# Block attention of a decoder trunk: transposes of q, k and three groups' probabilities by VectorE blocks and on-chip transfers

## The chip, the cores and the metric

The kernel runs on one core of a Trainium2 chip. The core has a matrix engine (TensorE, PE; its weight loads are listed as PEld), VectorE (DVE), ScalarE (ACT), GpSimd (POOL) and SyncE (SP), which here only issues transfers. Each engine works through a fixed list of instructions in order; semaphores make one wait for another. Transfers are issued on queues of SP, ACT and POOL and carried out by 16 DMA engines. The on-chip memory (SBUF) has 128 partitions; PE writes to banks of a second memory, PSUM.

The metric is device time in microseconds (us), the median of the runs; the profile is of one execution.

## The reference

A trunk of two layers on one sequence of 256 positions, width 1024, all in float32. Each layer is half a SwiGLU FFN (width 2816), a token mixer, and another half FFN; each part has an RMS norm with a shift, a scale and a gate worked out from a vector c (here called modulations). The mixer of layer 0 is the block attention (16 heads of 64) that the change touches; that of layer 1 has its own low-rank attention and is left as it is.

```python
def moba_attention(h, w_qkv, q_g, k_g, w_o, rel_bias, positions):
    qkv = (h @ w_qkv).reshape(B, S, 3, H, Dh)
    q = rms_norm(qkv[:, :, 0], q_g).transpose(0, 2, 1, 3)
    k = rms_norm(qkv[:, :, 1], k_g)
    v = qkv[:, :, 2]
    ...
    s = jnp.einsum("bhqd,bhqnkd->bhqnk", qc, kg).astype(jnp.float32) * scale + bias.astype(jnp.float32)
    mask = (kidx <= qi[None, None, :, None, None]) & sv[None, None, :, :, None]
    s = jnp.where(mask, s, NEG)
    p = jax.nn.softmax(s.reshape(B, H, QC, nslot * L), axis=-1).reshape(s.shape).astype(vg.dtype)
    return jnp.einsum("bhqnk,bhqnkd->bhqd", p, vg)
    ...
    return o @ w_o
```

The block length is 256, the whole sequence, so what remains is causal attention over 256 keys with a bias by relative position.

## The kernel before

**Precision and weights.** Every large matrix product is made of three: each float32 operand is split in a high part (rounded to the faster float32r) and a low part (the rest), and high x high, high x low and low x high are summed in PSUM (`mm3`, lines 898 to 900). A weight tile (`wload`) comes from DRAM on SP's queue into `raw` (three buffers of 1 MB), ScalarE writes its high part `hi` (line 690), VectorE the low part `lo` (line 691), 1024 columns at a time, into eight buffers each. So all weights pass through ScalarE and VectorE too. The function `weight_tiles` fixes the order in which they come.

**Modulations.** VectorE also multiplies the modulation matrices with c, in units of one 512 KB tile `adaw` (lines 705 and 746; line 746 for the gates). They are spread over the stages by `ada_pace`, with a time to spread them over (`MOBA_PACE`, 98, in the block attention).

**The order of instructions.** The Python program emits the work in one order, helped by a clock of TensorE time: `pe(us)` moves the clock, `later(us, fn)` emits `fn` when the clock has moved so far, `until(cond)` emits what is pending until the condition holds. Then the class `Order` lays out every engine's list anew: it works out how long each instruction takes (`duration`), when it is needed (`needs`), and places all instructions one by one on five engines (`place`), with the buffers of each pool, a model of the DMA engines, and at most eight transfers of SP in flight. TensorE takes the earliest emitted instruction that is ready, the others the one needed first. `NUDGE` shifts four single instructions in this.

**Block attention (`moba`).** The heads go in four groups g of four (`GH`). `project` makes q and k of a group (512 columns) for a tile t of 128 positions (two tiles); `qk` normalises each head (squares on ScalarE, sum on VectorE at line 1309, the power -1/2 on GpSimd at line 1310, a multiply on VectorE at line 1458) into `qn`; `vals` makes v of two groups at once. The order is q/k of group 0 and v of groups 0 and 1, q/k of 1, v of 2 and 3, q/k of 2, q/k of 3. `to_T` transposes `qn` on TensorE (line 1478, eight 128x128 transposes per group) into PSUM, and ScalarE copies them out with the gains (line 1480) as `qT` and `kT`.

**One group (`attention`).** `scores` makes q times k into four PSUM banks (line 1206), VectorE adds the bias and finds the row's limit (line 1223), ScalarE takes exponentials with their sum (line 1230), VectorE multiplies by the reciprocals (line 1236). `transposes` turns the probabilities on TensorE (line 1245, twelve per group) and ScalarE copies them out as `pT` (line 1247). `av` multiplies with v (line 1271). For the first three groups `av` is kept (`glued`) and emitted at the head of the next group's `scores`. `load_bias` fetches the next group's bias on POOL's queue into its one buffer. At the end `out_proj` multiplies by the output weights in eight pieces of four k-slices; the first three pieces need groups 0 and 1 alone.

**Names of the instructions in the profile:** `tr` and `at` are PSUM tiles, `s` the probabilities, `bg` the bias, `h` and `oT` the split inputs of projections.

## Time and profile before

| | |
|---|---|
| median of 3 runs | 976.41 us (975.74 to 977.19) |
| the profiled execution, first to last instruction | 973.7 us |
| median less that span | 2.7 us |
| TensorE busy | 966.8 us, 99% |
| VectorE busy | 833.7 us, 86% |
| ScalarE busy | 597.9 us, 61% |
| GpSimd busy | 81.4 us, 8% |
| moved by DMA | 268.31 MB, mean 276 GB/s |

The page gives, for one execution, the busy time of each engine, 40 slices of the span, the DMA queues, the chain of work that ended last (followed back from the last instruction, at each step to what released it), the costliest groups of instructions by source line, and the DMA issues with their time to landing. The trace behind it is asked for windows of time, for the waits, the chain in order of time, and the timeline. A group's row reads: line, engine, operation, output<-input, shapes, count | busy us, mean ns of one | idle time of the engine before them and what ended it. TensorE's matmuls overlap, so the mean of one (about 390 ns) is longer than the distance from one to the next (about 228 ns).

The order of the stages: first FFN to about 207 us, block attention with its output projection to about 320 us, second FFN to about 507 us, the next layer's first FFN to about 700 us, then the second attention and, from about 790 us, the last FFN.

### The profile page before, as it was taken

Reading aid. Unit: us, or ns where it says so; the run is one execution under the profiler, and the core shown is the slowest. Engines: PE = TensorE matmul, PEld = TensorE weight load, DVE = VectorE, ACT = ScalarE, POOL = GpSimd, SP = SyncE. Lnnn points to the kernel's source line nnn. Section 1 sums busy time; section 2 is a strip of 40 time slices with the busy share of each in tenths; the row PEclk is TensorE's granted clock in tenths of the full one; section 3 lists DMA queues with packets and bytes.
Section 4 is the critical chain, followed back from the end, with each engine's and each line's share of the span. In section 5 each row is a group of like instructions: output and inputs, shape, how many; then the busy total and the mean of one; then the engine's idle time right before and its main releaser. Section 6 shows DMA issues by size and latency. Waiting matters only on the chain.

```text
span 973.7 us, 15174 instructions
## 1 busy us (share of the span) xinstructions
PE 966.8 (99%) x5562; PEld 829.1 (85%) x5566; DVE 833.7 (86%) x1397; ACT 597.9 (61%) x1082; POOL 81.4 (8%) x130
## 2 busy tenths in 40 slices
PE   8999999999999999999999999999999999999998
PEld 6998888888887888888888888888998888888887
DVE  7999999799999999999797699988998789666643
ACT  5689655377766955655367566543689696665521
POOL 2001100022230000000010000000142000000000
PEclk9999999999999999999999999999999999999999
DMA  9987989799887699999887598997634367545630
GB/s 355 408 339 262 335 314 384 281 359 360 303 302 246 226 351 348 331 327 346 318 306 269 191 345 330 362 373 241 202 120 165 131 259 276 200 173 195 237 131 22
DMA packets 56002, 268.31 MB, mean 276 GB/s; under 512 B 6638, under 2 KB 7864, under 8 KB 38008
## 3 DMA queue, kind: packets, MB, share of 16 engines
q1 hardware_dynamic: 53136, 259.23, 71.9%
q0 software_dynamic: 2352, 7.77, 2.5%
q8 instruction: 44, 0.72, 0.3%
q10 hardware_dynamic: 440, 0.34, 0.1%
q14 instruction: 30, 0.25, 0.1%
HBM read 263.09 MB, written 4.23 MB: 275 GB/s over the span
## 4 chain that ended last, share of the span: by engine, by line
PE 95%; DVE 2%; POOL 1%; DMA 1%; issue 1%; ACT 0%; SPq 0%; DVEq 0%; ACTq 0%
PE mm L1112 26%; PE mm L898 15%; PE mm L899 15%; PE mm L900 15%; PE mm L1120 14%; PE at L1198 1%; PE at L1245 1%; PE tr L1374 1%; POOL hr L1310 1%; PE at L1271 1%; PE mm L1847 1%; PE tr L948 1%; PE tr L1657 1%; PE mm L1848 1%; PE mm L1849 1%; PE tr L1847 1%
## 5 line engine op out<-in xcount | busy, mean ns | idle before, releaser
L691 DVE TENSOR_TENSOR lo<-raw,hi 128x1024 fp32r<-128x1024 f32 (+2 forms) x302 | 358.5, 1207 | 84.4 <-ACT hi L690 79.1
L690 ACT ACTIVATE hi<-raw 128x1024 fp32r<-128x1024 f32 (+2 forms) x302 | 305.9, 1044 | 137.1 <-PE mm L900 100.0
L1112 PE MATMUL mm<-h,hi 128*128 128x512 f32 x1104 | 266.7, 392 | 0.0
L1112 PEld LDWEIGHTS mm<-h,hi 128*128 128x128 f32 x1104 | 202.1, 188 | 39.1
L1120 PEld LDWEIGHTS mm<-h,lo 128*128 128x128 f32 x1104 | 142.5, 191 | 5.7
L1120 PE MATMUL mm<-h,lo 128*128 128x256 f32 x1104 | 145.5, 283 | 0.0
L705 DVE CUSTOM_DVE_ANT_0 adaw<-adaw,c_b,cols 128x1024 f32<-128x1024 f32 (+1 forms) x112 | 140.2, 1269 | 0.3 <-DMA adaw<-in_ada_dram 0.2
L898 PE MATMUL mm<-hi,gh 128*128 128x512 f32 (+1 forms) x356 | 138.2, 389 | 0.0
L899 PE MATMUL mm<-lo,gh 128*128 128x512 f32 (+1 forms) x356 | 137.9, 387 | 0.0
L900 PE MATMUL mm<-hi,gl 128*128 128x512 f32 (+1 forms) x356 | 137.6, 387 | 0.0
L1124 ACT ACTIVATE both<-mm 128x256 f32<-128x256 f32 x108 | 40.6, 380 | 99.3 <-PE mm L1120 99.1
L898 PE MATMUL mm<-hi,h 128*128 128x512 f32 (+2 forms) x256 | 98.2, 389 | 0.0
L899 PE MATMUL mm<-lo,h 128*128 128x512 f32 (+2 forms) x256 | 98.1, 385 | 0.0
L900 PE MATMUL mm<-hi,h 128*128 128x512 f32 (+2 forms) x256 | 97.6, 385 | 0.0
L900 PEld LDWEIGHTS mm<-hi,gl 128*128 128x128 f32 x356 | 66.9, 188 | 13.6
L899 PEld LDWEIGHTS mm<-lo,gh 128*128 128x128 f32 x356 | 66.9, 188 | 13.1
L898 PEld LDWEIGHTS mm<-hi,gh 128*128 128x128 f32 x356 | 66.8, 188 | 13.1
L746 DVE CUSTOM_DVE_ANT_0 adaw<-adaw,c_b,cols 128x1024 f32<-128x1024 f32 x48 | 60.5, 1278 | 0.0
L898 PEld LDWEIGHTS mm<-hi,h 128*128 128x128 f32 x256 | 48.0, 188 | 9.2 <-issue 1.2
L900 PEld LDWEIGHTS mm<-hi,h 128*128 128x128 f32 x256 | 48.0, 188 | 8.5 <-DVE h L914 0.2
L899 PEld LDWEIGHTS mm<-lo,h 128*128 128x128 f32 x256 | 48.1, 188 | 8.1
L1125 DVE TENSOR_TENSOR both<-both,mm 128x256 f32<-128x256 f32 x108 | 43.8, 417 | 9.5 <-ACT both L1124 9.3
(264 smaller groups left out, 1148.5 us busy)
## 6 DMA issues: line engine op xcount, KB each, us to landing
raw<-in_w_dram SPq DMA_DIRECT2D x140, 1024.0 KB, 5.6
adaw<-in_ada_dram SPq DMA_DIRECT2D x158, 512.0 KB, 5.7
raw<-in_w_dram SPq DMA_DIRECT2D x14, 512.0 KB, 4.3
raw<-in_first_dram SPq DMA_DIRECT2D x7, 512.0 KB, 9.6
raw<-in_first_dram SPq DMA_DIRECT2D x9, 384.0 KB, 9.6
bias_d<-bt SPq DMA_DIRECT2D x12, 256.0 KB, 6.2
gate<-gate_d POOLq DMA_DIRECT2D x6, 512.0 KB, 7.6
bg<-bias_d POOLq DMA_DIRECT2D x4, 768.0 KB, 7.1
```

The costliest lines, as they stand in the source:

```text
L690: nc.scalar.activation(hi, src, AF.Copy)
L691: nc.vector.tensor_tensor(lo, src, hi.bitcast(F32), op=ALU.subtract)
L705: nc.vector.tensor_tensor_reduce(wt[:, cs], wt[:, cs], c_b[:, cs], 1.0, at, op0=ALU.mult, op1=ALU.add, accum_out=m_cols[:, i, c:c + 1])
L746: nc.vector.tensor_tensor_reduce(wt, wt, c_b, 1.0, places["gates"][:, c:c + 1], op0=ALU.mult, op1=ALU.add, accum_out=g_cols[:, row, k:k + 1])
L898: nc.tensor.matmul(ps, lh, rh, start=start, stop=False)
L899: nc.tensor.matmul(ps, lh, rl, start=False, stop=False)
L900: nc.tensor.matmul(ps, ll, rh, start=False, stop=stop)
L1112: nc.tensor.matmul(ps, wh, hk_both(h, k).rearrange("p i t q -> p (i t q)"), start=k == 0, stop=False)
L1120: nc.tensor.matmul(ps[:, S:], wl, hk_both(h, k)[:, 0].rearrange("p t q -> p (t q)"), start=False, stop=k == KD - 1)
L1124: nc.scalar.activation(sums, ps[:, S:], AF.Copy)
L1125: nc.vector.tensor_tensor(sums, sums, ps[:, :S], op=ALU.add)
L1847: nc.tensor.matmul(ps, wh, hh, start=False, stop=False)
```

## The change

The q, k and the probabilities of groups 0 to 2 are no longer turned by TensorE. VectorE transposes all 32x32 blocks of a [128, 512] tile in one instruction (`turn_blocks`, reading every fourth element, so that the four rows of partitions that belong together end up side by side), and four transfers from SBUF to SBUF (`move_blocks`) carry the 32 partitions of each quarter to all 128. The q/k moves are issued on ScalarE's queue, the moves of probabilities on SP's. Group 3's probabilities are still turned by TensorE.

- The gains of q and k are multiplied into one vector and applied to q alone; ScalarE writes the scaled q into the buffer of the blocks, k is read where the transfer left it, in runs of 32 elements.
- In the turned groups the probabilities are scaled by ScalarE, one head at a time, instead of by VectorE.
- The probabilities, their blocks and the moved copy share one tag of two buffers of 128x1536 instead of five of 128x512; v has one buffer of two groups instead of two.
- The projections go q/k of 0, v of 0 and 1, q/k of 1, 2, 3, v of 2 and 3; the weights come in that order.
- `Order` follows access patterns over partitions, gives on-chip transfers a duration of their own, and counts only SP's transfers as in flight; the nudges are gone. The waits before `scores` (`SQ_WAIT`) and the pace of the modulations in this stage change.

```diff
+AVT_WAIT = 9.0
+SQ_WAIT = 12.0
+TURN_LAST = False
...
-MOBA_PACE = 98.0
+MOBA_PACE = 86.0
...
-                for g in (0, -1, 1, -2, 2, 3):
+                for g in (0, -1, 1, 2, 3, -2):
...
-NUDGE = ((6613, 30), (6710, 100), (6712, 10), (6762, -100))
+NUDGE = ()
...
+                if self.aps[k][0].tensor.space == self.aps[k][-1].tensor.space:
+                    dur = min(dur, 2200.0 + 2.0 * self.transfer(k) + (1500.0 if e == "Pool" else 0.0))
...
-                if e != "Pool":
+                if e == "SP":
                     flight.append(t + dur)
...
+    def turn_blocks(z, x):
+
+        nc.vector.transpose(z.rearrange("p j n b -> p n j b"), x.rearrange("p (n a j) -> p n j a", j=4, a=NB))
+
+    def move_blocks(queue, xT, z):
+
+        X = math.prod(z.shape[2:])
+        for i in range(4):
+            queue.dma_start(xT[:, i].rearrange("p n b -> p (n b)"), z[i * NB:(i + 1) * NB].rearrange("a j n b -> a (j n b)"))
...
+        turned = bias is not None and (g < NG - 1 or TURN_LAST)
...
+            if bias is not None:
+                whole_s.append(ap.tile([P, 4, 3 * GH, NB], F32, tag="w", name=nm("s"), bufs=2).rearrange("p i n b -> p (i n b)").rearrange("p (u c) -> p u c", c=512))
...
-                nc.vector.tensor_tensor(ss[u], ss[u], rs[:, :n, None].to_broadcast([P, n, P * (t + 1)]), op=ALU.mult)
+                if turned:
+                    for i in range(n):
+                        nc.scalar.activation(ss[u][:, i, :], ss[u][:, i, :], AF.Copy, scale=rs[:, i:i + 1])
+                else:
+                    nc.vector.tensor_tensor(ss[u], ss[u], rs[:, :n, None].to_broadcast([P, n, P * (t + 1)]), op=ALU.mult)
             state["s"] = g + 1
-            later(PT_WAIT, transposes)
+            if not turned:
+                later(PT_WAIT, transposes)
+                return
+            z, w = [ap.tile([P, 4, 3 * GH, NB], F32, tag="w", name=nm(n), bufs=2) for n in ("zP", "pT")]
+            for u in range(len(us)):
+                turn_blocks(z[:, :, u * GH:(u + 1) * GH, :], ss[u].rearrange("p e k -> p (e k)"))
+            move_blocks(nc.sync, w, z)
...
-        later(S_WAIT, scores)
+        later(S_WAIT if bias is None else SQ_WAIT, scores)
...
-                    v[g] = v[g + 1] = ap.tile([P, NT, 512], F32, tag="v", name=nm("v"), bufs=2)
+                    v[g] = v[g + 1] = ap.tile([P, NT, 512], F32, tag="v", name=nm("v"))
...
-                for i in range(2):
-                    pt = tr_tile()
-                    for t in range(NT):
-                        for j in range(GH // 2):
-                            nc.tensor.transpose(kslice(pt, 2 * j + t), kslice(qn[g, t], 2 * i + j), ident)
...
+                z = ap.tile([P, 4, 2 * GH, NB], F32, tag="zqk", name=nm("zqk"))
+                qkT = ap.tile([P, 4, 2 * GH, NB], F32, tag="qkT", name=nm("qkT"))
+                for t in range(NT):
+                    turn_blocks(z[:, :, t * GH:(t + 1) * GH, :], qn[g, t])
+                move_blocks(nc.scalar, qkT, z)
+                blocks = qkT.rearrange("p i (t n) b -> p t n i b", t=NT)
+                qT = z.rearrange("p j n b -> p (j n b)")[:, :GH // 2 * S].rearrange("p (t n q) -> p t n q", t=NT, q=P)
+                for t in range(NT):
+                    nc.scalar.activation(qT[:, t].rearrange("p n (i b) -> p n i b", b=NB), blocks[:, t, :GH // 2], AF.Copy, scale=gain)
...
-            for fn, g in ((qk, 1), (vals, 2), (qk, 2), (qk, 3)):
+            for fn, g in ((qk, 1), (qk, 2), (qk, 3), (vals, 2)):
```

More of the change, by code (lines that the diff above doesn't have):

```diff
@@ L350, in add @@
                     p0 = ap.offset // size
-                    p1 = p0 + ap.ap[0][1]
-                    key = ap.offset % size, tuple(tuple(d) for d in ap.ap[1:])
+                    p1 = p0 + 1 + sum(d // size * (c - 1) for d, c in ap.ap if d >= size)
+                    key = ap.offset % size, tuple(tuple(d) for d in ap.ap if d[0] < size)
                     if key not in masks:
@@ L1181, in attention @@
     def attention(ap, g, qTs, kTs, vs, bias, oT, state, after_s=None):
-        pT, ss, sms = {}, [], []
+        pT, ss, whole_s = {}, [], []
+        turned = bias is not None and (g < NG - 1 or TURN_LAST)
         us = UNITS if bias is None else SIDES
@@ L1212, in scores @@
             mxs = []
-            for (t, es), ps in zip(us, banks):
+            if bias is not None:
+                whole_s.append(ap.tile([P, 4, 3 * GH, NB], F32, tag="w", name=nm("s"), bufs=2).rearrange("p i n b -> p (i n b)").rearrange("p (u c) -> p u c", c=512))
+            for u, ((t, es), ps) in enumerate(zip(us, banks)):
                 nk = P * (t + 1)
-                s3 = ap.tile([P, 512], F32, tag="w", name=nm("s"), bufs=5).rearrange("p (e k) -> p e k", k=nk)
+                s3 = whole_s[0][:, u] if whole_s else ap.tile([P, 512], F32, tag="w", name=nm("s"), bufs=5)
+                s3 = s3.rearrange("p (e k) -> p e k", k=nk)
                 mx = small([P, 4], "mx")
@@ L1235, in scores @@
                 nc.vector.reciprocal(rs[:, :n], sm[:, :n])
-                nc.vector.tensor_tensor(ss[u], ss[u], rs[:, :n, None].to_broadcast([P, n, P * (t + 1)]), op=ALU.mult)
-            state["s"] = g + 1
-            later(PT_WAIT, transposes)
+                if turned:
[3 more added lines that the diff above has]
+                    nc.vector.tensor_tensor(ss[u], ss[u], rs[:, :n, None].to_broadcast([P, n, P * (t + 1)]), op=ALU.mult)
+            state["s"] = g + 1
+            if not turned:
[5 more added lines that the diff above has]
+            move_blocks(nc.sync, w, z)
+            for u, (t, es) in enumerate(us):
+                for i, e in enumerate(es):
+                    for kb in range(t + 1):
+                        pT[t, e, kb] = w[:, :, u * GH + i * (t + 1) + kb, :]
+            turned_in()
         def transposes():
+            if whole_s:
+                pw = ap.tile([P, 4, 3 * GH, NB], F32, tag="w", name=nm("pT"), bufs=2)
+                pw = pw.rearrange("p i n b -> p (i n b)").rearrange("p (u c) -> p u c", c=512)
             for u, (t, es) in enumerate(us):
@@ L1245, in transposes @@
                         nc.tensor.transpose(kslice(pt, i * (t + 1) + kb), ss[u][:, i, kb * P:(kb + 1) * P], ident)
-                w = ap.tile([P, 512], F32, tag="w", name=nm("pT"), bufs=5)
+                w = pw[:, u] if whole_s else ap.tile([P, 512], F32, tag="w", name=nm("pT"), bufs=5)
                 nc.scalar.activation(w, pt, AF.Copy)
@@ L1253, in transposes, with turned_in @@
             pe(1.4)
+            turned_in()
+        def turned_in():
             state["p"] = g + 1
@@ L1259, in transposes @@
             else:
-                later(AV_WAIT, lambda: av([1] if g == NG - 1 else [0, 1]))
+                later(AVT_WAIT if turned else AV_WAIT, lambda: av([0, 1] if turned or g < NG - 1 else [1]))
         def av(ts):
@@ L1427, in moba @@
             load_bias(0)
-            gains = {n: places[n] for n in ("moba_q", "moba_k")}
-            nc.vector.tensor_scalar(gains["moba_q"], gains["moba_q"], -DH ** -0.5, None, op0=ALU.mult)
-            qT = ap.tile([P, GH // 2, S], F32, name="qT")
+            gain = places["moba_q"]
+            nc.vector.scalar_tensor_tensor(gain, gain, -DH ** -0.5, places["moba_k"], op0=ALU.mult, op1=ALU.mult)
             oTp = ap.tile([P, KD, 2, NT, P], F32R, name="oT")
@@ L1472, in to_T @@
                 until(lambda: state.get("s", 0) >= g)
-                kT = ap.tile([P, GH // 2, S], F32, tag="kT", name=nm("kT"))
-                for i in range(2):
-                    pt = tr_tile()
-                    for t in range(NT):
-                        for j in range(GH // 2):
-                            nc.tensor.transpose(kslice(pt, 2 * j + t), kslice(qn[g, t], 2 * i + j), ident)
-                    pv = pt.rearrange("p (j q) -> p j q", j=GH // 2)
-                    nc.scalar.activation((qT, kT)[i], pv, AF.Copy, scale=gains[("moba_q", "moba_k")[i]])
-                pe(0.9)
-                def half(x, e, n0, n1):
-                    return x[e % 2 * DH:(e % 2 + 1) * DH, e // 2, n0:n1]
+                z = ap.tile([P, 4, 2 * GH, NB], F32, tag="zqk", name=nm("zqk"))
[7 more added lines that the diff above has]
+                    nc.scalar.activation(qT[:, t].rearrange("p n (i b) -> p n i b", b=NB), blocks[:, t, :GH // 2], AF.Copy, scale=gain)
+                rows = lambda x, e: x[e % 2 * DH:(e % 2 + 1) * DH]
                 attention(
                     ap, g,
-                    lambda e, t: half(qT, e, t * P, (t + 1) * P),
-                    lambda e, n: half(kT, e, 0, n),
+                    lambda e, t: rows(qT, e)[:, t, e // 2],
+                    lambda e, n: rows(blocks, e)[:, :n // P, GH // 2 + e // 2],
                     lambda e, kb: v[g][:, kb, (g % 2 * GH + e) * DH:(g % 2 * GH + e + 1) * DH],
```

## The prediction

> **What bounds the kernel now.** I read the page first: the engines' busy time and the chain that ended last.
>
> ```profile
> PE 966.8 (99%) x5562; PEld 829.1 (85%) x5566; DVE 833.7 (86%) x1397; ACT 597.9 (61%) x1082; POOL 81.4 (8%) x130
> ...
> PE 95%; DVE 2%; POOL 1%; DMA 1%; issue 1%; ACT 0%; SPq 0%; DVEq 0%; ACTq 0%
> ```
>
> TensorE (PE) is busy in 966.8 of 973.7 us and holds 95% of the chain. An average hides the stages, so next come windows: the block attention with its output projection (207 to 320), the start of the second FFN, the rest of that FFN's first part, and its down projection with the next FFN's first matmuls. Columns: stretch, length, then busy time of PE, PEld, VectorE (DVE), ScalarE (ACT) and POOL, granted clock, DMA share, GB/s.
>
> ```profile
> 207.00:320.00 113.00, 112.84 (x646) 91.65 (x645) 106.69 (x213) 81.92 (x172) 24.96 (x16) 1.00 0.83 302
> 320.00:344.00 24.00, 24.00 (x113) 19.67 (x113) 21.96 (x35) 21.93 (x42) 1.48 (x1) 1.00 0.73 275
> 344.00:445.00 101.00, 101.00 (x584) 89.15 (x583) 97.26 (x145) 59.01 (x92) 2.23 (x4) 1.00 0.91 338
> 445.00:529.00 84.00, 84.00 (x382) 69.36 (x381) 70.11 (x96) 47.31 (x73) 2.94 (x2) 1.00 0.82 302
> ```
>
> In the stage of the change PE idles 0.16 us in 113: time comes off only if PE work comes off. But VectorE idles just 6.3 us there and 3.7 us in the next 101, and the DMA engines are 83% and 91% busy. PE gets relief; the work goes to the two resources with the least room. Then the chain of waits, in order of time (start, length, what), inside the stage:
>
> ```profile
> 232.23 0.87 PE tr L1478 x8
> ...
> 235.85 1.51 PE at L1206 x16
> ...
> 237.79 0.23 PE mm L899
> ...
> 243.03 1.31 PE at L1245 x12
> ...
> 256.15 1.51 PE mm L1271 x24
> ...
> 300.37 1.51 PE at L1206 x16
> ...
> 310.93 1.08 PE at L1271 x16
> ```
>
> These are, for one group of four heads: q/k transposes, scores, one matmul of a projection, transposes of the probabilities, their product with v; then the last group's scores and final product.
>
> **The change part by part.** The groups of instructions of the stage (207 to 325), one row for each shape: busy us, mean ns | idle before.
>
> ```profile
> L746 DVE CUSTOM_DVE_ANT_0 adaw<-adaw,c_b,cols 128x1024 f32<-128x1024 f32 x8 | 10.0, 1278 | 0.0
> ...
> L1236 DVE TENSOR_TENSOR s<-s,rs 128x512 f32<-128x512 f32 x12 | 8.2, 691 | 0.3
> ...
> L1247 ACT ACTIVATE pT<-at 128x512 f32<-128x512 f32 x12 | 6.6, 597 | 2.8 <-PE at L1245 2.8
> ...
> L943 ACT ACTIVATE y<-x,rstd 128x256 f32<-128x256 f32 x8 | 3.6, 495 | 0.0
> ...
> L1480 ACT ACTIVATE qT<-tr,cols 128x512 f32<-128x512 f32 x4 | 2.8, 689 | 2.6 <-PE tr L1478 2.6
> L1480 ACT ACTIVATE kT<-tr,cols 128x512 f32<-128x512 f32 x4 | 2.7, 681 | 0.0
> ...
> L913 ACT ACTIVATE h<-y 128x128 fp32r<-128x128 f32 x5 | 1.5, 307 | 0.1
> ```
>
> *PE, removed.* The q/k transposes of all groups go, four blocks of 0.87 (x8), and those of three groups' probabilities, three blocks of 1.31 (x12). 3.48 + 3.93 = 7.4 us, all on the path: PE has no idle time to absorb them. *PE, changed.* Scores and products now read moving operands in runs of 32 elements. No row shows such a matmul. Bounds: nothing, or twice the blocks of 1.51 (four of scores, three of products: +10.6 us). I take nothing, since the element count is unchanged and every matmul row here goes by its count.
>
> *VectorE.* Removed: nine of the twelve multiplies L1236, 9 x 0.69 = 6.2. Added: 2 block transposes for each of four groups and 3 for each of three, 17 of 128x512. The trace has none. The nearest row of that size is L1236 itself, 0.69; I take it: 11.7, net +5.5. The reads step over four elements, so the ceiling comes from two reductions of the same 128 elements, strided (L1343) and contiguous (L1356):
>
> ```profile
> L1343 DVE TENSOR_REDUCE own<-ident 128x32 f32<-128x128 f32 x1 | 0.4, 374 | 0.0
> ...
> L1346 DVE CAST posq<-posi 128x256 f32<-128x256 int32 x1 | 0.3, 285 | 0.0
> L1356 DVE TENSOR_REDUCE blk<-ident 128x4 f32<-128x128 f32 x1 | 0.3, 272 | 0.0
> ```
>
> 102 ns more over 128 elements is 0.8 ns for each; over 512, +0.41: 1.10 apiece, 18.7 in all, net +12.5. The floor is twice the conversion of 256 elements (row L1346), 0.57: 9.7, net +3.5. At 0.69 the stage asks VectorE for 106.7 + 5.5 = 112.2 us where PE now asks for 105.4. The cover is the modulation work of L746, 10.0 us for a gate that is read only behind the next FFN's down projection; 445 to 529 has 13.9 us of VectorE idle to take it. If it isn't put off, 6.8 us land on the path.
>
> [...]
>
> *ScalarE.* Removed: 8 x 0.69 (L1480) + 9 x 0.60 (L1247) = 10.9. Added: 8 scaled q copies at L943's 0.495 = 4.0; 24 scalings of the probabilities, 12 x 0.307 and 12 x 0.495 = 9.6; the issue of 16 transfers. An issue on SP reads 0.33:
>
> ```profile
> 306.51 0.33 SPq L838 DMA_DIRECT2D raw<-in_w_dram  x1
> 309.76 4.07 SPq L722 DMA_DIRECT2D adaw<-in_ada_dram  x3
> ```
>
> so 5.3, between nothing and, by the second row's 4.07 for three, 21.8. I take the single issue, which contains no wait. Net +8.0 on 81.9 of 113: it fits in 105 (floor +2.7; ceiling +24.5, which fills it). The wait: behind a move that waits for its block transposes stand ScalarE's weight splits, and VectorE's behind those; the splits made ahead cover it, and if that cover is gone a late transpose costs what it is late, up to a 0.69 or two.
>
> *Transfers.* Four moves of 512 KB for q/k, on ScalarE's queue, three of 768 KB for the probabilities on SP's, each in four parts: 4.3 MB, 14 us at 302 GB/s in a stage whose share is 0.83 of 113. 93.8 + 14 = 108: full, unless the same gate loads (eight of 512 KB, 4.2 MB) go later. Landing times (us, last column), nearest in size:
>
> ```profile
> adaw<-in_ada_dram SPq DMA_DIRECT2D x158, 512.0 KB, 5.7
> raw<-in_w_dram SPq DMA_DIRECT2D x14, 512.0 KB, 4.3
> ...
> gate<-gate_d POOLq DMA_DIRECT2D x6, 512.0 KB, 7.6
> bg<-bias_d POOLq DMA_DIRECT2D x4, 768.0 KB, 7.1
> ...
> out_dram<-x SPq DMA_DIRECT2D x3, 256.0 KB, 2.0
> ```
>
> Ends 2.0 (quiet engines) and 7.6 (by which a step below overruns by 2.1 instead of 0.9, and the sum ends at 973.2). For the probabilities I take 6.4, halfway between 5.7 (same queue) and 7.1 (same size); for q/k 5.7. On SP's queue the weight loads stand behind a move that waits for VectorE. They already wait there mostly for VectorE, so I charge nothing; the ceiling is 2.1, three transposes for the weights of one group.
>
> *The loop of one group.* Now the last exponential of group 0 begins at 239.95, 4.1 after its scores:
>
> ```profile
> 239.95 0.49 ACT L1230 ACTIVATE s<-s,mx 128x256 f32<-128x256 f32 x1
> ```
>
> It ends at +4.6; then 4 x 0.307 + 4 x 0.495 = 3.2 of scaling, a last block transpose 0.69, the move 6.4: +14.9, where today the PE transposes run from +7.2. Since the product of group g stands in front of the scores of g+1, and s, its blocks and their moved copy share two buffers, a step can't be shorter. PE's work in a step: two projections of 24 matmuls at 0.23, 11.0, with scores and product 1.51 each: 14.0. Overrun 0.9 us in two steps (1 to 2, 2 to 3); the first hides, because group 1's q/k come later than that anyhow. 1.8 us.
> *q/k path*: two block transposes 1.4, move 5.7, q copy 1.0 = 8.1 instead of today's 3.6 (transposes at 232.23 to scores at 235.85). With q/k projected first, a group's wait is behind 11.0 us of the next projection. Cost nothing; without that cover 4.5 us a group.
> *Last group* keeps PE transposes; scores to final product 10.6 us (300.37 to 310.93). In front stand 3 of 8 output pieces (12 matmuls, 2.8 us each) and, once group 2 is in, one more and the first halves of four: enough. *v in one buffer instead of two*: its copy waits for group 1's product, with the second v projected last; nothing. *POOL*: the bias loads keep their order, nothing; if one blocks a reciprocal root behind it, the next q/k pays, at most the 7.1 of its landing. *The four nudges dropped, the pace 98 to 86*: they shift order only; PE's 0.16 us of waits can only grow, by up to one step's overrun, 0.9; I take nothing.
>
> **Sum.** 7.4 - 1.8 = 5.6 us. The profiled execution spans 973.7, which gives 968.1; the median of the runs is 976.4, 2.7 more around the span, so 970.8.
>
> **The rivals.**
> *All of it arrives*: moves land by 5.5 us and no step overruns: 976.4 - 7.4 = 969.0. For it: PE has other work at every point. Against: two steps have under 1 us to spare by my own count. 0.18.
> *The debt* (the change doesn't bring what it removes): VectorE's 6.8 us and the full DMA engines are not put off, and the next FFN, where VectorE idles 3.7 us in 101, waits for weight splits. 7.4 - 6.8 = 0.6: 975.8, from 974 to 978. At 1.10 for a transpose, the strided row's ceiling, 7 us more are asked and the 10.0 of put-off work no longer covers: 6.8 + 7.0 - 10.0 = 3.8 lost, with 0.41 longer in each of four loops, 1.6, and 1.8 as before: 976.2, the same place. This second way has 0.10 of the chance. [...] For it: the rows of VectorE. Against: 13.9 us free later. 0.24.
> *Slower: the moves land late.* SP's queue carries megabyte loads in front of the moves; at 302 GB/s one is 3.5 us. Each us over 5.5 (14.0 less the 8.5 in front of the move) costs two steps, so it decides at 5.5 + 7.4/2 = 9.2 us. With one load in front, 9.9: 2 x 4.4 = 8.8 lost, 977.8. With two, 13.4, the first step joins too (its product comes 20.3 us after its scores, 256.15 against 235.85, so from 11.8): 2 x 7.9 + 1.6 = 17.4 lost, 986.4. For it: PE's order is fixed beforehand, so every late move stops it. Against: the loads themselves land in 5.7, so little usually stands in front. 0.15, and 0.03 more for slow strided operands.
>
> **How the numbers follow.** My forecast has 0.40, with its own range 969 to 973.2. Within 0.2%, about 2 us, nothing can be told from no change: 974.5 to 978.3. Faster: 0.40 + 0.18 + 0.06 of the debt = 0.64; same: 0.13 of the debt + 0.01 of late moves; slower: 0.05 of the debt + 0.14 + 0.03 = 0.22. The range 968.2 to 980.5 leaves out the two-load case and the strided operands, about 0.12, and little below, since no more than 7.4 us of PE work goes.
>
> **What would show it.** Right: no PE blocks on q/k, a PE count lower by 68, PE idle in the stage of 1 to 3 us ended by the moves in front of groups 1 and 2's products; block transposes near 0.69; landings near 6; gate work slid past 345. Wrong: transposes above 1 us; landings above 9; PE waiting in 330 to 445 for splits; score blocks longer than 1.51.

## The result and the profile after

The changed kernel takes 981.41 us (median; 980.87 to 982.04) beside 976.18 (975.74 to 977.19) for the kernel before: ratio 1.0054, 95% interval 1.0043 to 1.0064. It is 5.2 us slower, where 5.6 us less were forecast, and just above the forecast range. The profiled execution spans 979.6 us, 5.9 more than before. Ratios here and below leave out single executions at a lower granted clock (one of a kernel below took 1059 us at a clock of 0.85).

The page, engines' busy time and the chain that ended last:

```profile
PE 964.6 (98%) x5498; PEld 826.0 (84%) x5498; DVE 842.3 (86%) x1405; ACT 600.2 (61%) x1097; POOL 81.9 (8%) x130
...
PE 90%; DMA 3%; DVE 3%; ACT 2%; issue 1%; POOL 1%; ACTq 0%; DVEq 0%
```

TensorE is still busy for nearly the whole span, but its share of the chain fell from 95% to 90%; transfers, VectorE and ScalarE took what it lost. The same four windows as before (stretch, length, busy PE, PEld, DVE, ACT, POOL, granted clock, DMA share, GB/s):

```profile
207.00:320.00 113.00, 103.55 (x554) 83.22 (x553) 101.53 (x195) 78.55 (x177) 25.11 (x15) 0.95 0.88 302
320.00:344.00 24.00, 24.00 (x115) 19.31 (x115) 22.58 (x40) 22.81 (x47) 3.02 (x2) 1.00 0.61 228
344.00:445.00 101.00, 101.00 (x577) 88.83 (x576) 98.20 (x143) 59.60 (x92) 1.16 (x2) 1.00 0.92 334
445.00:529.00 84.00, 84.00 (x389) 69.53 (x388) 71.55 (x104) 47.56 (x75) 4.01 (x4) 1.00 0.85 318
```

The loss lies in the attention stage alone: TensorE stands 9.45 us there (0.16 before), at a mean clock of 0.95; behind it nothing waits. What TensorE waits for in that stage (total us, times, longest):

```profile
PE mm L1311 <- DMA pT<-zP: 8.5, 2, 5.9
PE mm L1311 <- ACT hi L695: 0.6, 1, 0.6
PE at L1222 <- ACT zqk L1520: 0.4, 1, 0.4
```

The products wait for the moved probabilities, of group 0 (5.9 us) and of group 1. The new instructions in the groups of the stage (busy us, mean ns of one | idle before):

```profile
L1183 DVE STREAM_TRANSPOSE zP<-s 128x512 f32<-128x512 f32 x9 | 9.2, 1060 | 0.0
L1183 DVE STREAM_TRANSPOSE zqk<-qn 128x512 f32<-128x512 f32 x8 | 8.6, 1084 | 0.0
```

and the moves' parts among the transfers (count, KB of each, median us from issue to landing):

```profile
pT<-zP SPq DMA_DIRECT2D x12, 192.0 KB, 3.8
...
qkT<-zqk ACTq DMA_DIRECT2D x16, 128.0 KB, 5.0
```

A block transpose takes 1.06 to 1.08 us, not 0.69. The chain of waits shows what this made of group 0, from the normalised q and k to its product, and where the last turned group ends (start, length, what):

```profile
232.20 0.69 DVE qn L1497
...
233.79 1.07 DVE zqk L1183
...
234.88 0.66 ACTq L1189
...
237.21 6.30 DMA qkT<-zqk
...
248.39 0.69 DVE hv L1349
249.07 1.13 DVE lo L696
250.20 0.20 DVE s L1242
...
255.17 7.46 DMA raw<-in_w_dram
...
262.65 3.75 DMA pT<-zP
...
266.54 2.85 PE mm L1311 x24
...
304.39 1.55 PE mm L1311 x24
305.94 1.51 PE at L1222 x16
```

The four parts of the q/k move are issued one after another from 234.88 and the last lands at 243.51: 8.6 us. Scores follow at 245.2 (235.85 before), yet VectorE first adds the bias to them at 250.20, since it had fallen behind. Its timeline, with ScalarE's, shows why (start, length, what, [idle before <- what ended it]):

```profile
243.62 0.91 ACT L1520 ACTIVATE zqk<-qkT,cols 128x256 f32<-128x256 f32 x2 [3.24 <-DMA qkT<-zqk]
245.51 1.22 DVE L696 TENSOR_TENSOR lo<-raw,hi 128x1024 fp32r<-128x1024 f32 x1 [3.57 <-ACT hi L695]
```

ScalarE stands 3.24 us at its copy of the moved q, and the weight splits (hi) are behind that copy in its queue; so VectorE stands 3.57 us for a split, and then has three of its own (lo), a normalisation and a reduction (hv) in its queue before the bias. The late q and k thus delay group 0's probabilities too. No run tests this alone; in e2 below, where TensorE still turns q and k, group 0's loop from scores to product is 18.4 us. The probabilities' last part is issued at 262.65, by the chain after the landing of a weight load issued at 255.17, and the product starts at 266.54: 21.3 us after its scores. The product itself takes 2.85 us for 24 matmuls that take 1.55 at 304.39: behind the wait of 5.9 us the granted clock is 0.50 (the windows under "The slow clock").

So much for TensorE's own account: 7.4 us of work gone, 9.45 us of waits, and some 3 us of slow matmuls (an estimate: 6.4 us of work at a clock of 0.50, to 269.7 us behind the first wait and to 290.15 behind the second) come to +5. Which of these causes which is what the experiments ask.

### The profile page after: what moved, and what is told of

Its sections match the earlier page's. It is cut to its first block, busy times and chain, and to the rows that moved or that the text cites. A ratio compares the mean times of both kernels' runs of the same rounds, so it can differ in the third digit from the quotient of the medians.

```text
span 979.6 us, 15131 instructions
## 1 busy us (share of the span) xinstructions
PE 964.6 (98%) x5498; PEld 826.0 (84%) x5498; DVE 842.3 (86%) x1405; ACT 600.2 (61%) x1097; POOL 81.9 (8%) x130
## 4 chain that ended last, share of the span: by engine, by line
PE 90%; DMA 3%; DVE 3%; ACT 2%; issue 1%; POOL 1%; ACTq 0%; DVEq 0%
PE mm L1117 26%; PE mm L1125 14%; PE mm L903 13%; PE mm L905 13%; PE mm L904 13%; DMA raw<-in_w_dram 1%; DMA qkT<-zqk 1%; PE at L1214 1%; DVE lo L696 1%; PE tr L1414 1%; PE at L1311 1%; PE tr L1694 1%; PE at L1282 1%; PE mm L1886 1%; PE mm L1885 1%
```

## The experiments

Theory A: TensorE's order is fixed with durations that are too short (0.69 for a transpose, a third of a microsecond for an issue, landings under light load), so late moves stop it; with B to N as rivals and refinements. Ratios are to the kernel before, run on the same chip.

| kernel | turned by blocks | transposes read | queues per move | durations in the order | us | ratio, 95% interval |
|---|---|---|---|---|---|---|
| changed | q, k, P | every 4th column | 1 | as changed | 981.41 | 1.0054, 1.0043–1.0064 |
| e3_order_only | nothing | – | – | as changed | 976.68 | 1.0006, 0.9997–1.0015 |
| e1_qk_blocks_only | q, k | every 4th | 1 | as changed | 982.90 | 1.0070, 1.0058–1.0083 |
| e2_p_blocks_only | P | every 4th | 1 | as changed | 978.09 | 1.0016, 1.0007–1.0026 |
| e4_plan | q, k, P | every 4th | 1 | measured | 979.95 | 1.0046, 1.0032–1.0059 |
| e5_no_moves | q, k, P, not moved | every 4th | – | as changed | 974.82 | 0.9993, 0.9984–1.0001 |
| e6_contiguous_timed | q, k, P | neighbours | 1 | as changed | 978.99 | 1.0025, 1.0016–1.0034 |
| e9_no_moves_contiguous | q, k, P, not moved | neighbours | – | as changed | 968.94 | 0.9924, 0.9912–0.9936 |
| e7_fill | as changed, waits filled | every 4th | 1 | as changed | 981.64 | 1.0064, 1.0050–1.0077 |
| e8_p_two_queues | P | every 4th | 2 | measured | 976.26 | 1.0006, 0.9998–1.0015 |
| e10_qk_two_queues | q, k | every 4th | 2 | as changed | 976.65 | 1.0005, 0.9996–1.0013 |
| e11_two_queues_plan | q, k, P | every 4th | 2 | measured | 980.93 | 1.0041, 1.0029–1.0053 |
| e12_p_sorted | P | neighbours | 2 | measured | 977.82 | 1.0027, 1.0015–1.0038 |
| e13_full_sorted_plan | q, k, P | neighbours | 2 | measured | 981.01 | 1.0052, 1.0039–1.0065 |
| e14_full_sorted | q, k, P | neighbours | 2 | as changed | 982.60 | 1.0075, 1.0063–1.0087 |
| e15_qk_sorted | q, k | neighbours | 2 | measured | 972.78 | 0.9968, 0.9956–0.9980 |
| e16_full_sorted_load | q, k, P | neighbours | 2 | under load | 974.81 | 0.9983, 0.9974–0.9992 |
| e17_no_p_moves | q, k, P; P not moved | neighbours | 2 | measured | 970.89 | 0.9948, 0.9935–0.9962 |

### Which part of the change costs: order, q and k, or probabilities

```diff
# e3: everything turned by TensorE again; e1: the first line alone; e2: the second part alone
-        turned = bias is not None and (g < NG - 1 or TURN_LAST)
+        turned = False
...
-                for t in range(NT):
-                    turn_blocks(z[:, :, t * GH:(t + 1) * GH, :], qn[g, t])
-                move_blocks(nc.scalar, qkT, z)
...
+                            nc.tensor.transpose(kslice(pt, 2 * j + t), kslice(qn[g, t], 2 * i + j), ident)
```

Order alone: 

> The changed kernel's order of projections, buffers, pace and counts, with every transposition back on TensorE. Theory A (the changed kernel loses because transposes, issues and landings take longer than the order that is fixed when the kernel is built allows for, so that TensorE stands in front of the products of attention): all these waits are gone, 975 to 977.5 us, as before the change. Rival B (the new order, the fewer score and value buffers and the dropped hand adjustments cost the time): 979 to 982 us, as the changed kernel. Rival C (q/k moves on ScalarE's queue) and rival D (VectorE and the transfers are saturated in the stage) say as A.

q and k alone: 

> q and k by blocks and moves, probabilities by TensorE. TensorE has 3.5 us less than before. Theory A: the chain from q and k to the scores is 9 us longer than before but TensorE waited only 0.4 us at the scores in the changed kernel: 973 to 977 us, clock in the stage above 0.98. Rival C (the moves on ScalarE's queue and the splits held up behind them are the cost): 979 us or more. Rival B: 976 to 979 us (its 4 to 5 us less 3.5). Rival D (VectorE): 976 to 979 us, with waits of TensorE in the feed-forward stages.

Probabilities alone: 

> Probabilities of three groups by blocks and moves, q and k by TensorE as before. TensorE has 3.9 us less than before. Theory A: the products still wait for moves that land some 2 us (group's moves 6.5 us from first issue to landing against 4.4 in the order's own reckoning) plus 1.1 us (three transposes) later than planned, so 3 us each for up to three groups: 974 to 980 us, with TensorE idle in front of the products. Rival C: the loss goes with the q/k moves, 970 to 973 us. Rival B: 976 to 979 us without waits for the moves.

e3 stands level with before, so rival B falls: projecting q and k first, the fewer buffers, the pace and the dropped adjustments cost nothing measurable. e2 loses 1.6 us, inside Theory A's band (974 to 980): its two waits in front of products (2.0 and 1.6 us) eat nearly all of the 3.9 us that TensorE is relieved of. e1 was a surprise: with less work moved it is slower than the whole change, against Theory A's 973 to 977 and as rival C said. TensorE's waits in e1's stage:

```profile
PE at L1222 <- ACT zqk L1520: 4.3, 2, 2.8
PE at L1282 <- DVE rs L1254: 2.0, 2, 1.8
```

The scores do wait for the moved q and k. In the whole change TensorE waits only 0.4 us there; that the products' waits hold it back until q and k are in is likely, but no run parts it.

### The order's durations

```diff
# e4; occ is what an issue holds the queue, dur the time to landing
-                    dur = min(dur, 2200.0 + 2.0 * self.transfer(k) + (1500.0 if e == "Pool" else 0.0))
+                    dur, occ = (5500.0 if e == "Activation" else 4200.0), 650.0
...
+        elif "Transpose" in kind:
+            d = 30.0 + 2.0 * n
```

> The changed kernel, but its order is worked out with what its own trace shows: 1.05 us for a block transpose, 0.65 us of the queue for each on-chip move, 5.5 us (q, k) and 4.2 us (probabilities) from issue to landing. Its own reckoning then ends 6.0 us later than the changed kernel's own did (967.5 against 961.4), and 0.9 us before that of the kernel before. Theory A: 974 to 977.5 us, waits in front of the products of a group 4 us or less each, clock in the stage above 0.98. Rival B: 979 to 982 us. Rival C: unchanged, 979 to 982 us, since the moves stay on ScalarE's queue. Rival D: 978 us or more, with VectorE late in the stages behind.

Of 5.3 us lost, 0.8 came back (the intervals overlap). 979.95 misses Theory A's band of 974 to 977.5 and lies in the 979 to 982 of rivals B and C, of which B had fallen with e3. Two products still waited, 6.9 us in all, the longer one 4.2 us. These better durations alone don't mend it.

### Without the moves, without the stride

```diff
# e5
-                move_blocks(nc.scalar, qkT, z)
-                blocks = qkT.rearrange("p i (t n) b -> p t n i b", t=NT)
...
+                blocks = z.rearrange("p i (t n) b -> p t n i b", t=NT)
...
-            move_blocks(nc.sync, w, z)
# e6 (and e9 = both)
-        nc.vector.transpose(z.rearrange("p j n b -> p n j b"), x.rearrange("p (n a j) -> p n j a", j=4, a=NB))
+        nc.vector.transpose(z.rearrange("p j n b -> p n j b"), x.rearrange("p (n j a) -> p n j a", j=4, a=NB))
```

> The changed kernel without its on-chip moves: block transposes stay, and scores and the three products read the blocks where they lie, so the part of the computation that puts blocks in their partitions is left out. Theory A (issue and landing of the moves are what TensorE stands for): no wait of TensorE in front of scores or products over 0.7 us, the 7.4 us of TensorE come out nearly whole, 968 to 971.5 us. Rival D (eight plus nine block transposes at 1.05 us on VectorE, and the scaling on ScalarE, are too much for the stage): 973 us or more, with VectorE named in front of TensorE's waits.

e6 asks whether the stride makes the price of a block transpose, which was 1.03 to 1.11 us in the changed kernel:

> The changed kernel with block transposes that read 32 neighbouring columns instead of every fourth one, so what lands in the partitions is permuted. [...] Time: within 2 us of the changed kernel if the price is the same, up to 4 us less if it falls.

> The changed kernel without its on-chip moves and with block transposes of 32 neighbouring columns (0.69 us instead of 1.06): the placing of blocks in their partitions and the order inside a block row are left out. Without the moves alone the time was 974.8 us, with TensorE standing 4 us for VectorE late in the stage. Theory G (what was left there is VectorE's extra 0.37 us times 17 transposes, 6.3 us, in a stage where it has little slack): 969 to 972 us, and no wait for VectorE over 1 us. Rival H (the other added work, ScalarE's scaling and copies and the order itself, is what is left): 973.5 to 975.5 us.

> As the look at contiguous block transposes (moves kept, placing inside a block row left out), now timed: that look had 977.7 us in one run against 981.4 us for the changed kernel. Theory G: 977 to 979 us, so the stride of four costs about 3.5 us of the changed kernel's loss. Rival: 980.5 us or more, the look was a fast draw.

Neighbouring columns, the groups of e6's timed kernel, same shapes as above:

```profile
L1183 DVE STREAM_TRANSPOSE zP<-s 128x512 f32<-128x512 f32 x9 | 6.1, 694 | 0.3 <-ACT s L1257 0.3
L1183 DVE STREAM_TRANSPOSE zqk<-qn 128x512 f32<-128x512 f32 x8 | 5.5, 695 | 0.0
```

e5, e6, e9 and, below, e17 leave out a part of the computation (placing the blocks, their order, or both): they show what the rest costs, and are no versions to use. The stride costs 0.37 us in each of 17 transposes, 6.3 us of VectorE. e5 was expected at 968 to 971.5 us and came out at 974.8: without any move, TensorE waited for VectorE's half of the split of the last turned group's output instead.

```profile
PE mm L905 <- DVE oT L919: 3.2, 1, 3.2
PE mm L903 <- ACT oT L918: 0.8, 1, 0.8
```

That is what Rival D said (973 or more, with VectorE named), and e9 settles it: without moves and stride the stage has no TensorE wait left (113.00 busy of 113.00) and the time falls by 0.76%, 7.4 us, the whole of what the forecast took off TensorE. At 968.94 it lies at the lower end of Theory G's 969 to 972.

```profile
207.00:320.00 113.00, 113.00 (x611) 90.40 (x610) 108.63 (x220) 90.01 (x199) 27.29 (x17) 1.00 0.79 283
```

In ratios: the stride costs 0.69% (6.7 us) without moves (e5 against e9) and 0.29% (2.8 us) with them (changed against e6); the moves cost 0.61% with the stride (changed against e5) and 1.01%, 9.9 us, without (e6 against e9). The two hide one another in part, as two late inputs of the same chain would. In e6 the moves' parts also land later (median 5.2 us for P and 6.4 for q/k, against 3.8 and 5.0), which may be why only 2.8 us show; this wasn't parted. The first run of contiguous transposes gave 977.7 us; timed, it was 979.0, at the end of Theory G's band.

### The slow clock

```diff
# e7, in front of the products of groups 0 and 1
+            for _ in range((24, 9, 0, 0)[g] if bias else 0):
+                nc.tensor.matmul(flat, spare[0], spare[1], start=True, stop=True)
```

> The changed kernel with 24 idle matmuls of 512 columns (0.227 us each, 5.4 us) in front of the product of group 0 and 9 (2.0 us) in front of that of group 1, into the bank that the product then overwrites, where TensorE stood for 5.9 and 2.5 us. Theory A with its second half (after a wait of over 2 us TensorE is granted half its clock for some 5 us, which costs about 3 us in two places): product of group 0 takes 1.5 to 1.6 us instead of 2.85, granted clock above 0.95 between 260 and 275 us, 976.5 to 979.5 us. Rival E (the blocks behind the wait are slow because of the transfers or of their strided operands): no change, 981 to 982.5 us, product 2.5 us or more.

Three windows of 4 us behind the first wait, of the changed kernel:

```profile
260.00:264.00 4.00, 0.62 (x3) 0.19 (x1) 4.00 (x6) 3.24 (x4) 0.53 (x1) 0.86 0.99 342
264.00:268.00 4.00, 1.46 (x14) 1.49 (x16) 3.72 (x5) 2.33 (x4) 2.03 (x1) 0.50 0.97 321
268.00:272.00 4.00, 4.00 (x34) 3.13 (x31) 2.01 (x12) 2.04 (x8) 1.64 (x1) 0.79 0.97 393
```

and of e7:

```profile
260.00:264.00 4.00, 4.00 (x19) 3.30 (x19) 4.00 (x7) 3.42 (x4) 0.11 (x1) 1.00 0.97 353
264.00:268.00 4.00, 3.04 (x27) 2.38 (x27) 3.87 (x5) 2.36 (x5) 2.45 (x1) 1.00 1.02 291
268.00:272.00 4.00, 4.00 (x36) 3.13 (x32) 3.20 (x19) 2.96 (x12) 1.64 (x1) 1.00 0.92 361
```

and, from e7's chain of waits, the products of groups 1 and 2:

```profile
285.68 1.58 PE mm L1328 x24
...
304.27 1.55 PE mm L1328 x24
```

The mechanism was right: with TensorE kept busy the clock stays at 1.00 and the products take 1.55 to 1.58 us (so strided operands cost nothing, against the cause that rival E named). Its price was wrong: the time didn't move, and lies in rival E's 981 to 982.5. Group 2's scores start 2.5 us earlier than in the changed kernel (287.19 against 289.70), yet its product starts at 304.27, as it did at 304.39 with the slow clock; the faster TensorE only waited longer there, 2.8 us. What leads to the moved probabilities sets the pace there, not TensorE.

### Two queues

```diff
# e8, e10 and all below
-            queue.dma_start(xT[:, i].rearrange("p n b -> p (n b)"), z[i * NB:(i + 1) * NB].rearrange("a j n b -> a (j n b)"))
+            (nc.sync if i % 2 else nc.scalar).dma_start(xT[:, i].rearrange("p n b -> p (n b)"), z[i * NB:(i + 1) * NB].rearrange("a j n b -> a (j n b)"))
```

> Probabilities by blocks and moves, q and k by TensorE; the four moves alternate between SyncE's and ScalarE's queue, and the order is worked out with measured durations (1.05 us a block transpose, 0.65 us an issue, 4.5 us to landing). Theory A: issue takes 1.3 us instead of 2.6, the products' waits (2.0 and 1.6 us with one queue and the old durations) fall below 0.7 us each, TensorE saves its 3.9 us: 971.5 to 974.5 us, faster than before the change. Rival F (ScalarE, with the exps, the scaling and now issues, gets late, or SyncE's loads are held up): 975.5 us or more.

> q and k by blocks and moves, probabilities by TensorE (982.9 us with the four moves of a group on ScalarE's queue, one after the other), now two moves on ScalarE's and two on SyncE's queue. Theory A (the path from q and k to the scores, 12 to 14 us against 11 us of TensorE's own cover, is what is paid, of which 2.6 us are issue in series): 1.3 us less in three groups, 978.5 to 981.5 us. Rival C (ScalarE's queue, whose splits stand behind the issues and the copies): 976 to 978 us. Rival I (landing alone sets it, or SyncE's queue holds its two moves behind loads): 982 us or more.

> The whole change, with each move's four parts on both queues and the order worked out with measured durations (1.05 us, 0.65 us, 4.5 us to landing); its own reckoning ends at 966.3 us, 2.0 us before that of the kernel before and 1.2 us before that with one queue each. Theory A (only the durations and the serial issue were wrong): 974 to 976.5 us. Theory G (VectorE's 17 strided transposes keep their price in a stage without slack, and landings lengthen with the load on the transfers): 976.5 to 980 us.

e10 gained 6.3 us over e1, in rival C's band rather than Theory A's. The first q/k move of e1 on ScalarE's timeline:

```profile
235.13 2.85 ACTq L1189 DMA_DIRECT2D qkT<-zqk  x4
238.02 2.01 ACT L695 ACTIVATE hi<-raw 128x1024 fp32r<-128x1024 f32 x2 [5.42 <-DVE m_cols L710]
243.73 0.91 ACT L1520 ACTIVATE zqk<-qkT,cols 128x256 f32<-128x256 f32 x2 [3.69 <-DMA qkT<-zqk]
```

and of e10:

```profile
234.68 1.34 ACTq L1189 DMA_DIRECT2D qkT<-zqk  x2
236.06 2.01 ACT L695 ACTIVATE hi<-raw 128x1024 fp32r<-128x1024 f32 x2 [3.94 <-DVE m_cols L710]
240.29 0.91 ACT L1520 ACTIVATE zqk<-qkT,cols 128x256 f32<-128x256 f32 x2 [2.22 <-DMA qkT<-zqk]
```

From first issue to the copy that reads it: 8.6 us on one queue, 5.6 on two. Of the 3.0 us, 1.5 are issues and the other half landing: the last part landed 6.3 us after its issue in e1 and 4.8 in e10. That isn't so for the probabilities, where a part's median to landing is 3.6 us on one queue (e2) and 5.1 and 5.4 on two (e8). The copy then holds ScalarE 1.5 us less (3.69 against 2.22 us idle), so both theories have a share in it. e8 stands level with before, in rival F's band (975.5 or more): its waits (0.9 and 2.5 us) still ate most of TensorE's 3.9. And both halves together, e11, lose 4.5 us although each by itself is level; 980.93 is above the bands of both its theories.

### Without the stride, computing the same

```diff
# P: ScalarE's scaling writes sorted columns (e12, e13, e14, e16, e17)
-                        nc.scalar.activation(ss[u][:, i, :], ss[u][:, i, :], AF.Copy, scale=rs[:, i:i + 1])
...
+                        o = sorted_s[0][:, u, i * nk:(i + 1) * nk].rearrange("p (b j a) -> p b a j", j=4, a=NB)
+                        nc.scalar.activation(o, ss[u][:, i, :].rearrange("p (b a j) -> p b a j", j=4, a=NB), AF.Copy, scale=rs[:, i:i + 1])
...
# q, k: the normalisation reads PSUM with a step, in two halves (e13 to e17)
+                for i in range(2):
+                    nc.vector.tensor_tensor(
+                        x.rearrange("p (n j h a) -> p h n j a", j=4, h=2, a=16)[:, i],
+                        ps.rearrange("p (n h a j) -> p h n j a", h=2, a=16, j=4)[:, i],
...
```

> Probabilities by blocks and moves on two queues, q and k by TensorE, as the version that stood level with before the change (976.3 us), but ScalarE's scaling writes every fourth column together, so that VectorE's transposes read 32 neighbouring columns and what arrives is the same. Theory G (VectorE's stride price): 9 times 0.37 us less on VectorE in a stage where it has little slack, 973 to 975.5 us. Rival J (the landings, 5 to 8 us, hold the products whatever VectorE does): 975.8 to 977 us. If ScalarE pays for writing with a step what VectorE paid for reading (its 256-column scaling over 0.6 us instead of some 0.4): 976 us or more.

> The whole change, computing the same, without strided transposes: ScalarE's scaling and the two halves of the q/k normalisation write the columns in sorted order; two queues for each move; order with measured durations (it ends at 964.1 us, 4.2 us before that of the kernel before). Theory G: without the stride the whole change gains, 971 to 975 us. Rival J: the moves of q, k and probabilities are in each other's way on the two queues and with the loads, 976.5 to 981 us as with strided transposes (980.9).

> As the one before, but with the order's old durations for the moves (0.33 us an issue and 3.0 to 3.4 us to landing), so that only transposes and queues differ from the changed kernel. If the order's durations matter: 2 us or more above the version with measured durations, with TensorE standing for moves. If not (the chain is what it is): within 1 us of it.

> q and k by blocks and moves on two queues (976.65 us with strided transposes), probabilities by TensorE, with the q/k normalisation writing sorted columns in two halves so that the transposes read neighbouring columns. Theory G: 8 times 0.37 us less on VectorE, less some 0.1 us a half for the extra instruction: 974 to 976 us. Rival J: 976 to 977.5 us.

e15 is the fastest version that computes the same, and beats both kernels: 972.8 us, 3.1 less than before of the 3.5 that four q/k blocks are worth, with next to no wait:

```profile
207.00:320.00 113.00, 112.73 (x632) 91.62 (x631) 107.55 (x223) 83.33 (x181) 23.87 (x16) 1.00 0.85 299
```

(It is better than Theory G's 974 to 976, and differs from e10 in the stride and in the order's durations; the two weren't parted.) For the probabilities the stride only changed hands. Scaling writes in e12, where in the changed kernel 256 columns took 0.495 us and 128 took 0.388:

```profile
L1264 ACT ACTIVATE sj<-s,rs 128x256 f32<-128x256 f32 x12 | 6.9, 737 | 0.0
...
L1264 ACT ACTIVATE sj<-s,rs 128x128 f32<-128x128 f32 x12 | 4.8, 506 | 0.0
```

0.24 + 0.12 us for each of 12 pairs, 4.3 us, against 3.3 saved on VectorE. e12 loses, as the last sentence of its expectation allowed for (scaling over 0.6 us, 976 or more); that the two stand in series on the path of the same group is argued from the code. e13 is at the end of Rival J's band, and e14 is 1.6 us above it, between its two forecasts: moving the stride from VectorE to ScalarE and the normalisation mended nothing while both kinds of moves are there (e6, where no instruction paid for the sorting, was 2.8 us better). Theory G falls for this version of the whole change.

### What is left: the order under load, and the probabilities' moves

```diff
# e16 against e13, the durations of the order alone
-                    dur, occ = (4500.0 if e == "Activation" else 4500.0), 650.0
+                    dur, occ = (6000.0 if str(self.aps[k][-1].tensor.name).startswith("pT") else 5500.0), 650.0
# e17 against e13
...
-            move_blocks(nc.sync, w, z)
+            w = z
```

> The whole change with sorted columns and two queues (981.0 us), its order worked out with the landings as they were under load in that run: 6.0 us for a part of the probabilities' moves and 5.5 us for q and k, instead of 4.5. The order's own reckoning ends at 964.2 us, as with 4.5. Theory K (the order only lacked the durations under load): the products' waits of 0.9, 3.1 and 3.0 us shrink below 1 us each, 973 to 976.5 us. Rival L (with both kinds of moves in the stage each path is longer than TensorE's work beside it, whatever order is fixed): 978 to 982 us, waits at other places.

> The whole change with sorted columns and two queues for q and k, but without the moves of the probabilities: the product reads the blocks where they lie, so their placing is left out. Theory M (what is left of the loss is the landing of the probabilities' moves alone, q and k's half pays as it did by itself): 968.5 to 971.5 us, no wait of TensorE over 1 us. Rival N (ScalarE's sorted writing, 0.24 us more for 256 columns, and the longer chain of the groups are too much also without these moves): 973 us or more.

TensorE's waits in e13:

```profile
PE mm L1319 <- DMA pT<-s: 7.0, 3, 3.1
PE at L1225 <- ACT zqk L1531: 1.6, 2, 1.3
PE mm L905 <- ACT oT L920: 0.8, 1, 0.8
```

and in e16:

```profile
PE at L1225 <- ACT zqk L1531: 2.7, 2, 1.7
PE mm L905 <- ACT oT L920: 1.9, 2, 1.0
PE mm L1319 <- DMA pT<-s: 0.7, 2, 0.4
```

With nothing but other durations, the same instructions take 974.8 instead of 981.0 us. The order now puts the next group's scores ahead of a product in all three steps, e13's in two of three; what else in it saved time wasn't parted. So Theory K holds and rival L falls: the whole change can gain, if only 1.2 us of its 7.4, since 5.3 us of waits remain. e17 takes them down to 2.0 us and ends at 970.9, in Theory M's band (though one wait is 1.3 us, where M said none over 1): of what is lost, most goes with the probabilities' moves. Whether that is their landing, their issues or their load on the transfers isn't parted. e14 to e13 to e16, the same edit under three sets of durations, span 7.8 us, more than the 7.4 us of TensorE. But one order was built for each set, so how much an order changes the time by chance isn't known: e4's other durations gave 0.8 us, and e3's other order nothing measurable.

## Why the prediction was wrong, step by step

**TensorE's 7.4 us**: right, and shown whole by e9. *Strided operands of TensorE, nothing*: right, 1.55 us for a product and 1.51 for scores at full clock. *Order, buffers, nudges and pace, nothing*: right (e3).

**VectorE's 0.69 for a block transpose**: wrong; 1.06 to 1.08, near the ceiling of 1.10 that the strided reduction had given. The choice went to the row of equal size, which reads neighbours, instead of to the strided one. It cost 2.8 us here, and would have cost 6.7 of the 7.4 had the moves been free. The same transpose of neighbours takes 0.69 (e6), so 0.37 us of each go with the stride; by what mechanism, no run shows.

**The issue at 0.33, no wait**: wrong twice. A part of a move holds its queue 0.63 to 0.65 us (median), and four stand in series: 2.6 to 3.3 us that the sum put on no path.

**Landing 5.7 for q/k, 6.4 for P**: group 0's P move was right, 6.5 us (259.94 to 266.40); its q/k move took 8.6, the others 4.5 to 7.0.

**The loop of one group, 14.9 us**: this is the step that failed most in the whole change. It was 21.3 us for group 0, 17.6 for group 1 and 14.7 for group 2. The sum carried over the last exponential at +4.6 from the trace of before; here the exponentials ended at 254.7, 9.4 us after the scores, because VectorE's queue had other work in front of the bias. That was "the splits made ahead cover it", which failed as well: ScalarE's splits stood behind the late q/k copy (3.24 us), VectorE stood 3.57 us for them, and took up the bias 5 us after the scores. A path through three engines' queues isn't made from an earlier trace's distances when the change feeds those queues. The overrun of 1.8 us became 8.5 us of waits in front of the products.

**The q/k path, 8.1 us, "cost nothing" under a cover of 11.0**: it took 12.3 us (232.89 to 245.2), more than the cover. e1 shows what that costs when the products don't wait for moves: 6.5 us slower than before, although TensorE has 3.5 less to do.

**Not foreseen**: that TensorE's clock can fall around a wait. In the changed kernel it is 0.50 from 262.9 to 269.7 us, about the end of the wait of 5.9 us, and from 286.74 to 290.15, from the end of the one of 2.5. In e11 sixteen score matmuls behind a wait of 1.8 us took 2.57 us instead of 1.58, while e13 has a clock of 1.00 behind a wait of 3.1 (277 to 285 us) and 0.50 behind waits of 3.0 and 0.8 (305 to 309). The length of the wait in front doesn't decide it alone. e7 shows that it cost nothing by itself.

**The rivals**: *the moves land late* named the mechanism, a fixed order that every late move stops, but set its point at 9.2 us from issue to landing, which assumed all else in the loop as forecast; P's moves took 6.5 and were late by what stood in front of them. *The debt* was real in its second way alone, the transposes at 1.10: e5 shows it without the moves, and in e9, which has transposes at 0.69 and no moves either, TensorE has no wait in the stage, so the first way didn't occur there. It fell due inside the stage, not in the next FFN, where TensorE had no wait; that e5's 974.8 us is near the 975.8 forecast is chance, since that sum had other terms. Of the signs, the transposes over 1 us said "wrong", and that was so. Landings above 9, waits in 330 to 445 and score blocks longer than 1.51 at full clock didn't come. Waits in front of products and gate work slid past 345 came as forecast, but the waits were at groups 0 and 1, not 1 and 2, and 8.5 us instead of 1 to 3.

**Open**: why e11 loses 4.5 us where its halves are level. e16 shows that an order exists in which the whole doesn't lose; whether e11's loss (4.9 us of waits at scores, 3.7 at products) is its order or the moves beside one another wasn't parted. Landing points to q/k at most: a part's median rose from 3.8 to 3.9 us in e10 to 5.0 to 5.1 in e11, while the probabilities' 5.2 to 5.5 were 5.1 to 5.4 in e8 already. Second buffers for the q/k blocks weren't tried, and neither was a q/k copy that doesn't stand in front of the weight splits.

## What to carry to other kernels

Moving work off a busy engine can lengthen a path (q and k to scores: 3.6 us before, 12.3 after): add up that path in the new queues, with every issue in series, and hold it against the cover of the engine that waits, before counting the work saved. When an order is fixed beforehand, give it the durations of the loaded machine; the same instructions differed by 7.8 us under three sets of them (one order built for each). Try a move's parts on two queues where the issues hold up other work on the queue: it helped q and k on ScalarE's (8.6 to 5.6 us) and did little for the probabilities (ratio 1.0016 in e2, 1.0006 in e8, which has other durations too). Look for an instruction that can sort the columns at little cost (VectorE's normalisation, two halves of 0.41 us against 0.67 in one) before paying a stride; where none can, the stride only changes hands (ScalarE's scaling of 256 columns, 0.74 us against 0.50).

## What the hardware showed that was not expected

- A block transpose of 128x512 reading every fourth column takes 1.06 to 1.08 us (changed kernel), reading neighbours 0.69 (e6). ScalarE writing every 32nd column takes 0.74 us for 256 (e12), against 0.50 (changed kernel). VectorE reading PSUM with the same step of four paid little here: two halves of a normalisation at 0.41 us each (e13, e15) against 0.67 in one (changed kernel).
- A second queue shortened one kind of move and not the other: the first q/k move took 8.6 us from first issue to use on one queue (e1) and 5.6 on two (e10); a part of the probabilities landed in a median of 3.6 us on one (e2) and 5.1 and 5.4 on two (e8).
- In the changed kernel the granted clock fell to 0.50 for 6.8 us about the end of a wait of TensorE of 5.9 us, and for 3.4 us from the end of one of 2.5; in e13 it was 0.50 from 305 to 309 us, behind waits of 3.0 and 0.8. It stayed at 1.00 around waits of 2.0 (e2), 2.8 (e7) and 3.1 (e13).
